# Differential heads: one split over a bank's 128 rows, with DMAs placing the quarters

## The chip, the cores and the metric

The kernel runs on one core of a Trainium2 chip. The metric is the device time of one execution in microseconds (us). Engines are named TensorE (PE in the rows; PEld is its weight load), VectorE (DVE), ScalarE (ACT), GpSimd (POOL) and SyncE (SP), which here only issues DMAs.

## The reference

One decoder layer over x of 1 x 512 x 1024 float32: RMSNorm, one input projection whose columns go to four groups of four heads (MoBA, NSA, differential, sliding window), output projection, norm, residual, then a gated feed-forward part with a short convolution. The change touches the differential heads alone:

```python
dq4 = _heads(dq, GROUP_HEADS); dk4 = _heads(dk, GROUP_HEADS)   # (b, 4, s, 64)
# q1, k1 = the first 32 of 64 columns, q2, k2 = the last 32
s1 = einsum('bhqd,bhkd->bhqk', q1, k1) * 32 ** -0.5 - slope * dist
s2 = einsum('bhqd,bhkd->bhqk', q2, k2) * 32 ** -0.5 - slope * dist
p = _masked_softmax(s1, mask) - lam * _masked_softmax(s2, mask)
o = einsum('bhqk,bhkd->bhqd', p, v)                             # then an RMSNorm per head
```

So there are eight narrow heads of 32 columns, two for each of the four heads.

## The kernel before, in words

Every float32 operand is split in two: a rounded high part and the rest. A product of two operands is three matmuls, high by high, high by low and low by high.

The attention half has two kinds of work. The heads' own steps (scores, softmax, transposes, probabilities times values) are written in an order with due times and get a high priority. The projections that later heads need are "filler": a generator, `everything`, runs `fill_moba`, `fill_nsa`, `fill_diff`, `fill_swa` and `fill_out` in this order, some pieces between any two steps of the heads. One unit of filler, `fm_unit`, takes a split weight, fills one PSUM bank with the tag "mm" (there are two such banks) by 24 matmuls of 128x512, and returns it. The bank holds 128 projected columns as rows, by 512 positions. What must be done to it on ScalarE, VectorE and by DMA goes to a queue `side`, from which steps are taken one after another as the filler goes on; `mm_bank` makes sure that the steps of the bank before last have been written down. The splits of weights (lines 152 and 157) go through the same queue. A scheduler then plans the order of instructions on each engine from priorities and from when it believes that operands and buffers are ready.

`fill_diff` makes four such banks: for p = 0 and 1, the queries of heads 2p and 2p + 1, then the keys. The 128 rows of a bank are four quarters of 32 rows, one for each narrow head. For every quarter `narrow_stack` fills a tile "dd" of 128 x 512, of which 96 rows are used: the high part twice and the low part once, in such an order that one score matmul with a depth of 96 (line 1062) adds up all three products. In the kernel before, ScalarE writes the high part of one quarter (line 828), SP issues a DMA that copies it to its second place (line 829), and VectorE writes the low part (line 833): four times for each bank. The "dd" tiles share 18 buffers with other head tiles (tag F); the "sum" tiles are two buffers that the feed-forward weights use later (line 177).

SP also issues the loads of weights (lines 91 and 104) and of the gains (line 869), in the same queue as the copies.

Of the kernel before, what the change touches and what calls it, by code (L numbers as in the profile page):

```python
# [11 lines left out]
F32 = mybir.dt.float32  # L12
BF16 = mybir.dt.bfloat16
F32R = mybir.dt.float32r
AF = mybir.ActivationFunctionType
ALU = mybir.AluOpType
AX = mybir.AxisListType

S = 512
# [10 lines left out]
def f32(ap):  # L30
    return ap.bitcast(F32)
# [199 lines left out]
def kernel(  # L231
# [6 lines left out]
    vec, act, pool, pe, sp = nc.vector, nc.scalar, nc.gpsimd, nc.tensor, nc.sync  # L238
# [4 lines left out]
    wst = ctx.enter_context(tc.tile_pool(name="wst", bufs=4))  # L243
    vpool = ctx.enter_context(tc.tile_pool(name="big", bufs=BIGS))
    first_half = ExitStack()
    tab = first_half.enter_context(tc.tile_pool(name="tab", bufs=1))
# [5 lines left out]
    def nm(s):  # L252
        cnt[0] += 1
        return f"{s}_{cnt[0]}"
# [3 lines left out]
    def bank(tag):  # L258
        if tag == "pv":
            turn[0] ^= 1  # L260
            tag = ("va", "vb")[turn[0]]
        return psum.tile([128, 512], F32, tag=tag, name=nm(tag), bufs=1 if tag[0] == "v" else 2)

    def tt(name, tag="F"):
        return acts.tile([128, S], F32R, tag=tag, name=nm(name), bufs={"F": FB, "M": MB, "H": HB}[tag])
# [17 lines left out]
    def later(*fs):  # L283
        side.extend(fs)
        asked[0] += len(fs)
# [129 lines left out]
    for n in range(2):  # L415
        ps = bank("sc")
        for _ in range(WARM[n]):
            keep(pe.transpose(ps[:, 0:128], ident, ident))
        if n == 0:
            ps = bank("tr")  # L420
# [39 lines left out]
    def mm_done():  # L460
        marks.append(asked[0])

    def fm_unit():
        w = W.take()
        ps = mm_bank()
        yield from fm_pieces(ps, w, hT, slice(0, S))
        W.free()
        return ps
# [65 lines left out]
    def qscale(m, h, dim):  # L534
        return float(-np.float64(dim) ** -0.5 / np.float64(SLOPES[4 * h + m]))
# [59 lines left out]
    ps = bank("tr")  # L595
# [24 lines left out]
    pool.memset(pair, 0.0)  # L620
    pool.memset(pair[0:64, 0:1], 1.0)
    pool.memset(pair[64:128, 1:2], 1.0)
    nsink = tab.tile([128, 4], F32, name="nsink")
    keep(vec.tensor_scalar(nsink, sink, -1.0, None, ALU.mult))
    lprod = tab.tile([128, 2, 32], F32, name="lprod")
# [14 lines left out]
    nq, nk, dq, dk, sq_, sk = [], [], [], [], [], []  # L640
    vcs, cmp_, late = {}, {}, {}

    def tm_units(v, v3, n, extra=None):
        ws = [W.take() for _ in range(4)]
        for t in range(4):
            ps = mm_bank()
            sl = slice(128 * t, 128 * t + 128)
            for k in range(8):
                wh, wl = ws[k // 2]
                mm3(ps[:, 0:n], hT[0][k][:, sl], hT[1][k][:, sl], wh[:, k % 2, :], wl[:, k % 2, :], k == 0, k == 7)  # L650
                if t == 3 and k % 2:
                    W.free()
                yield 1
            later(*v_steps(ps, v, v3, t, (lambda ps=ps, t=t: extra(ps, t)) if extra else None))
            mm_done()
# [161 lines left out]
        vec.tensor_sub(ct[1], ps, f32(ct[0]))  # L817
        cmp_["v"], cmp_["p"] = vc, ct

    def narrow_stack(ps, scales, places, twice, put):  # L820


        ts_ = []

        def hi(c):
            t = tt("dd")
            ts_.append(t)
            act.activation(t[0:32], ps[32 * c:32 * c + 32, :], AF.Copy, scale=scales[c // 2])
            sp.dma_start(f32(t[twice:twice + 32]), f32(t[0:32]))

        def lo(c):
            t = ts_[c]
            vec.scalar_tensor_tensor(t[places:places + 32], ps[32 * c:32 * c + 32, :], scales[c // 2], f32(t[0:32]),
                                     ALU.mult, ALU.subtract)
            put.append(t)
        return [lambda f=f, c=c: f(c) for f, c in ((hi, 0), (hi, 1), (lo, 0), (hi, 2), (lo, 1), (hi, 3), (lo, 2), (lo, 3))]

    def fill_diff():
        for p in range(2):
            ps = yield from fm_unit()  # L840
            later(*narrow_stack(ps, [qscale(2, 2 * p + a, 32) for a in range(2)], 32, 64, dq))
            mm_done()
            ps = yield from fm_unit()
            later(*narrow_stack(ps, [1.0, 1.0], 64, 32, dk))
            mm_done()
        vcs["d"] = vpool.tile([128, 4, 512], F32R, tag="v", name="vd")
        vs = vpool.tile([128, 4, 512], F32R, tag="v", name="vs")
        vcs["s"] = vs[:, :, 0:384].rearrange("p t (n d) -> p t n d", n=2)
        yield from tm_units(vcs["d"], vcs["s"], 384)
        yield "diff"  # L850
# [37 lines left out]
    def everything():  # L888
        yield from fill_moba()
        yield from fill_nsa()  # L890
        yield from fill_diff()
        yield from fill_swa()
        yield from fill_out()
# [585 lines left out]
```

## Time and profile before

| | |
|---|---|
| median of 3 runs | 822.89 us (821.38 to 822.95) |
| the profiled execution | 821.32 us, of it 819.5 us span |
| mean granted TensorE clock | 0.984 of full speed |
| TensorE busy | 781.0 us (95% of the span) |
| VectorE busy | 665.6 us (81%) |
| ScalarE busy | 446.9 us (55%) |
| GpSimd busy | 338.5 us (41%) |

The shares are means over stages with different limits: an engine that is busy for 55% of the span can be the limit in a short stretch. The differential banks are written between 121.6 and 160.5 us, and their scores run from 159.2 to 234.3 us. Starts of instructions are microseconds from the start of the span.

### The profile page before, as it was taken

How to read it: one execution, taken by the hardware profiler on the slowest of the kernel's cores; microseconds unless marked ns; L12 is line 12 of the kernel's file. 1: busy time of each engine (PE TensorE's matmuls, PEld its weight loads, DVE VectorE, ACT ScalarE, POOL GpSimd, SP SyncE). 2: the span in 40 equal slices, each digit the busy share in tenths (PEclk: the TensorE clock that was granted, in tenths of full speed). 3: DMA queues.
4: the chain of work that ended last, by engine and by line, in shares of the span. 5: the costliest groups of instructions: out<-in, count | busy, mean ns of one | idle time of the engine just before them, and what ended most of it. 6: DMA issues, size and time to landing. Idle time of an engine off the chain costs nothing.

```text
span 819.5 us, 13505 instructions
## 1 busy us (share of the span) xinstructions
PE 781.0 (95%) x5087; PEld 712.1 (87%) x5087; DVE 665.6 (81%) x1131; ACT 446.9 (55%) x931; POOL 338.5 (41%) x309
## 2 busy tenths in 40 slices
PE   8999998999989769999999999999999999999995
PEld 8998986997868658988998998998998998998984
DVE  5657768877586999896797797897897987989857
ACT  6657666777676545645554453454454454445532
POOL 5245333336244757343343441461561561563103
PEclk9999999999989979999999999999999999999998
DMA  7455201416211403412114305216116026033212
GB/s 213 121 149 138 64 22 46 129 52 216 80 52 52 154 7 109 145 61 94 52 50 157 103 10 197 67 38 206 43 61 206 18 86 205 1 104 104 69 60 102
DMA packets 72920, 78.76 MB, mean 96 GB/s; under 512 B 7782, under 2 KB 58136, under 8 KB 72856
## 3 DMA queue, kind: packets, MB, share of 16 engines
q1 hardware_dynamic: 71032, 73.71, 29.3%
q10 hardware_dynamic: 1824, 4.20, 1.5%
q8 instruction: 40, 0.66, 0.3%
q14 instruction: 24, 0.20, 0.1%
HBM read 73.71 MB, written 2.10 MB: 93 GB/s over the span
## 4 chain that ended last, share of the span: by engine, by line
PE 57%; DVE 33%; issue 3%; DMA 3%; ACT 2%; POOL 1%; ACTq 0%; DVEq 0%; POOLq 0%
DVE wu L194 13%; PE mm L405 5%; PE mm L406 5%; PE mm L407 4%; DVE y L1362 3%; PE mm L1312 3%; PE mm L1314 3%; PE mm L1313 3%; PE tr L406 3%; PE tr L407 2%; PE sc L1314 2%; PE sc L1313 2%; PE sc L1312 2%; PE tr L405 2%; PE tr L973 2%
## 5 line engine op out<-in xcount | busy, mean ns | idle before, releaser
L194 DVE TENSOR_TENSOR wu<-pair,wu 128x512 fp32r<-128x512 f32 x188 | 174.6, 964 | 15.8 <-ACT wu L191 15.6
L191 ACT ACTIVATE wu<-pair 128x512 fp32r<-128x512 f32 x188 | 108.6, 622 | 76.3 <-PE sc L1314 19.8
L1314 PE MATMUL mm<-fT,wu 128*128 128x256 f32 x488 | 138.3, 283 | 0.7 <-DVE wu L194 0.7
L1312 PE MATMUL mm<-fT,wu 128*128 128x256 f32 x488 | 138.2, 283 | 0.7 <-ACT mo L1343 0.7
L1313 PE MATMUL mm<-fT,wu 128*128 128x256 f32 x488 | 138.2, 283 | 0.0
L1314 PE MATMUL sc<-fT,wu 128*128 128x256 f32 x392 | 111.3, 284 | 0.0
L1313 PE MATMUL sc<-fT,wu 128*128 128x256 f32 x392 | 111.1, 284 | 0.0
L1312 PE MATMUL sc<-fT,wu 128*128 128x256 f32 x392 | 111.0, 284 | 0.0
L152 ACT ACTIVATE wu<-raw 128x512 fp32r<-128x512 f32 (+2 forms) x126 | 71.3, 609 | 67.9 <-DMA raw<-in_ffn_w_down_dram 43.8
L177 POOL TENSOR_TENSOR sum<-pair 128x512 f32<-128x512 f32 x32 | 48.7, 1526 | 141.2 <-DMA pair<-in_ffn_w_up_dram 71.4
L177 POOL TENSOR_TENSOR pair<-sum,pair 128x512 f32<-128x512 f32 x32 | 56.2, 1771 | 116.6 <-DVE wu L194 114.7
L177 POOL TENSOR_TENSOR pair<-pair 128x512 f32<-128x512 f32 x64 | 103.4, 1628 | 2.0
L157 DVE TENSOR_TENSOR wu<-raw,wu 128x512 fp32r<-128x512 f32 (+2 forms) x96 | 73.5, 783 | 35.3 <-ACT wu L152 34.8
L1312 PEld LDWEIGHTS mm<-fT,wu 128*128 128x128 f32 x488 | 93.6, 192 | 1.2 <-ACT mo L1343 0.9
L1314 PEld LDWEIGHTS mm<-fT,wu 128*128 128x128 f32 x488 | 93.6, 192 | 0.9 <-DVE wu L194 0.9
L1313 PEld LDWEIGHTS mm<-fT,wu 128*128 128x128 f32 x488 | 93.6, 192 | 0.3
L941 POOL TENSOR_SCALAR P<-P,rc 128x128 f32<-128x128 f32 (+2 forms) x80 | 42.3, 547 | 84.3 <-DVE rc L1039 39.6
L1313 PEld LDWEIGHTS sc<-fT,wu 128*128 128x128 f32 x392 | 75.2, 192 | 0.3
L1312 PEld LDWEIGHTS sc<-fT,wu 128*128 128x128 f32 x392 | 75.2, 192 | 0.3
L1314 PEld LDWEIGHTS sc<-fT,wu 128*128 128x128 f32 x392 | 75.3, 192 | 0.0
L949 ACT ACTIVATE P<-P,mn 128x128 f32<-128x128 f32 (+2 forms) x96 | 52.1, 543 | 33.2 <-DVE mn L948 32.8
L157 POOL TENSOR_TENSOR wu<-raw,wu 128x512 fp32r<-128x512 f32 (+2 forms) x30 | 40.6, 1356 | 48.4 <-ACT wu L152 44.7
(318 smaller groups left out, 1955.8 us busy)
## 6 DMA issues: line engine op xcount, KB each, us to landing
pair<-in_ffn_w_gate_dram SPq DMA_DIRECT2D x16, 1024.0 KB, 7.7
pair<-in_ffn_w_up_dram SPq DMA_DIRECT2D x16, 1024.0 KB, 5.4
raw<-in_ffn_w_down_dram SPq DMA_DIRECT2D x32, 512.0 KB, 4.1
raw<-in_w_in_dram SPq DMA_DIRECT2D x14, 512.0 KB, 3.9
raw<-in_w_out_dram SPq DMA_DIRECT2D x8, 512.0 KB, 5.4
raw<-in_w_in_dram SPq DMA_DIRECT2D x10, 256.0 KB, 3.2
x<-in_x_dram SPq DMA_DIRECT2D x4, 512.0 KB, 4.6
x<-in_x_dram ACTq DMA_DIRECT2D x4, 512.0 KB
```

The lines of the kernel that those rows point to most:

```text
L152: keep(self.nc.scalar.activation(box["h"][:, sl], box["r"][:, sl], AF.Copy))
L157: keep(eng.tensor_tensor(box["l"][:, sl], box["r"][:, sl], f32(box["h"][:, sl]), op=ALU.subtract))
L177: self.nc.gpsimd.tensor_tensor(block(g, out), block(g, a), block(g, b), op=op)
L191: self.nc.scalar.activation(box["h"][g], block(g, src), AF.Copy)
L194: self.nc.vector.tensor_sub(box["l"][g], block(g, src), f32(box["h"][g]))
L405: pe.matmul(o, lh, rh, start=first, stop=False)
L406: pe.matmul(o, lh, rl, start=False, stop=False)
L407: pe.matmul(o, ll, rh, start=False, stop=last)
L949: act.activation(pi, pi, AF.Exp, bias=mn[:, i:i + 1], scale=-1.0, accum_out=sm[:, i:i + 1])
L1312: pe.matmul(o, wh, rh, start=first, stop=False, skip_group_check=True)
L1313: pe.matmul(o, wh, rl, start=False, stop=False, skip_group_check=True)
L1314: pe.matmul(o, wl, rh, start=False, stop=last, skip_group_check=True)
```

## The change

A bank is no longer split by quarters. ScalarE writes the high part of all 128 rows into a staging tile, VectorE the low part into another, and SP's DMAs carry the quarters to their places in the four "dd" tiles: eight copies of the high part and four of the low part for each bank. The staging tiles have the tag "sum". The scale of the queries differs between the two heads of a bank, so it becomes a column with a value for each row, filled by four memsets.

```diff
+    dscale = tab.tile([128, 2], F32, name="dscale")
+    for h in range(4):
+        pool.memset(dscale[64 * (h % 2):64 * (h % 2) + 64, h // 2:h // 2 + 1], qscale(2, h, 32))
...
-    def narrow_stack(ps, scales, places, twice, put):
-        ts_ = []
-
-        def hi(c):
-            t = tt("dd")
-            ts_.append(t)
-            act.activation(t[0:32], ps[32 * c:32 * c + 32, :], AF.Copy, scale=scales[c // 2])
-            sp.dma_start(f32(t[twice:twice + 32]), f32(t[0:32]))
-
-        def lo(c):
-            t = ts_[c]
-            vec.scalar_tensor_tensor(t[places:places + 32], ps[32 * c:32 * c + 32, :], scales[c // 2], f32(t[0:32]),
-                                     ALU.mult, ALU.subtract)
-            put.append(t)
-        return [lambda f=f, c=c: f(c) for f, c in ((hi, 0), (hi, 1), (lo, 0), (hi, 2), (lo, 1), (hi, 3), (lo, 2), (lo, 3))]
+    def narrow_stack(ps, scale, places, twice, put):
+        ts_ = [tt("dd") for _ in range(4)]
+        parts = [wst.tile([128, S], F32R, tag="sum", name=nm("parts"), bufs=2) for _ in range(2)]
+
+        def place(n, c, row):
+            sp.dma_start(f32(ts_[c][row:row + 32]), f32(parts[n][32 * c:32 * c + 32]))
+
+        def hi():
+            act.activation(parts[0], ps, AF.Copy, scale=scale)
+            for c in range(4):
+                place(0, c, 0)
+                place(0, c, twice)
+
+        def lo():
+            vec.scalar_tensor_tensor(parts[1], ps, scale, f32(parts[0]), ALU.mult, ALU.subtract)
+            for c in range(4):
+                place(1, c, places)
+                put.append(ts_[c])
+        return [hi, lo]
...
-            later(*narrow_stack(ps, [qscale(2, 2 * p + a, 32) for a in range(2)], 32, 64, dq))
+            later(*narrow_stack(ps, dscale[:, p:p + 1], 32, 64, dq))
...
-            later(*narrow_stack(ps, [1.0, 1.0], 64, 32, dk))
+            later(*narrow_stack(ps, 1.0, 64, 32, dk))
```

## Rows read from the trace of the kernel before

**Rows 1.** Busy time by windows: engines' busy us (instructions), PEclk, DMA share, GB/s

```profile
126.00:128.00 2.00, 0.65 (x4) 0.22 (x2) 1.94 (x3) 1.95 (x6) 1.00 (x1) 1.00 0.12 29
128.00:130.00 2.00, 1.46 (x7) 0.91 (x7) 2.00 (x8) 1.95 (x6) 0.00 (x0) 1.00 0.63 167
130.00:132.00 2.00, 1.36 (x5) 0.99 (x5) 1.96 (x5) 1.98 (x7) 0.00 (x0) 0.68 0.45 128
132.00:134.00 2.00, 1.93 (x5) 1.49 (x5) 1.91 (x8) 1.66 (x6) 0.00 (x0) 0.50 0.00 0
136.00:200.00 64.00, 64.00 (x358) 57.30 (x356) 48.63 (x124) 44.64 (x112) 31.71 (x38) 1.00 0.38 117
200.00:210.00 10.00, 8.75 (x41) 6.79 (x41) 8.00 (x22) 6.81 (x16) 2.30 (x3) 1.00 0.43 132
230.00:300.00 70.00, 53.31 (x282) 42.97 (x281) 59.59 (x130) 43.79 (x112) 38.18 (x43) 0.88 0.23 76
```

**Rows 2.** TensorE in order of time: start, us, instruction, idle before and releaser

```profile
109.66 0.47 PE L407 MATMUL mm<-hT,wu 128*128 128x512 f32 x1
...
124.68 0.39 PE L407 MATMUL mm<-hT,wu 128*128 128x512 f32 x1
...
128.19 0.33 PE L1005 MATMUL sc<-kk,qs 128*128 128x128 f32 x1 [1.54 <-DVE mn L948]
...
130.64 0.83 PE L973 MATMUL tr<-ident,P 128*128 128x128 f32 x3 [0.68 <-DVE PT L977]
...
132.18 0.79 PE L405 MATMUL mm<-hT,wu 128*128 128x512 f32 x1
```

**Rows 3.** The chain of waits around the first differential bank

```profile
123.50 0.69 DVE dd L833
...
125.94 0.68 DVE dd L833
...
130.73 0.69 DVE dd L833
131.43 0.70 DVE dd L833
```

**Rows 4.** Groups by line and form, 120 to 162 us: busy, mean ns, idle before

```profile
L828 ACT ACTIVATE dd<-mm 32x512 fp32r<-32x512 f32 x16 | 9.4, 589 | 3.2 <-DVE dd L833 2.7
...
L816 ACT ACTIVATE cmp<-vb 128x512 fp32r<-128x512 f32 x1 | 0.6, 597 | 0.0
...
L833 DVE SCALAR_TENSOR_TENSOR dd<-mm,dd 32x512 fp32r<-32x512 f32 x16 | 11.0, 687 | 2.2 <-ACT dd L828 1.8
...
L977 DVE TENSOR_TENSOR PT<-tr,PT 128x512 fp32r<-128x512 f32 x4 | 2.7, 685 | 0.3 <-ACT PT L976 0.2
```

**Rows 5.** The tile "dd": ns min/median/max, first and last start

```profile
L1062 PE MATMUL sc<-dd,dd x32: 221/338/502, 159.2 to 234.3; 96*128 96x128 f32 x8, 96*128 96x256 f32 x8, 96*128 96x384 f32 x8, 96*128 96x512 f32 x8
...
L829 SPq DMA_DIRECT2D dd<-dd x16: 507/510/609, 122.2 to 158.4; - x16
...
DMA to landing us min/median/max: 1.9/1.9/2.5
```

**Rows 6.** ScalarE in order of time

```profile
121.61 1.19 ACT L828 ACTIVATE dd<-mm 32x512 fp32r<-32x512 f32 x2
...
127.56 1.81 ACT L828 ACTIVATE dd<-mm 32x512 fp32r<-32x512 f32 x3
```

**Rows 7.** SP's DMA issues in order of time

```profile
127.61 0.91 SPq L91 DMA_DIRECT2D raw<-in_w_in_dram  x2
...
153.16 0.57 SPq L869 DMA_DIRECT2D gains<-in_attn_post_norm_dram  x1
...
158.43 0.51 SPq L829 DMA_DIRECT2D dd<-dd  x1
```

**Rows 8.** GpSimd in order of time, at the start

```profile
3.54 0.09 POOL L621 MEMSET pair<- 64x1 f32 x1
3.69 0.09 POOL L622 MEMSET pair<- 64x1 f32 x1
```

**Rows 9.** The tile "sum": ns min/median/max, first and last start

```profile
L177 POOL TENSOR_TENSOR sum<-pair x32: 1282/1664/1761, 191.0 to 747.7; 128x512 f32<-128x512 f32 x32
```

## The prediction, made before the kernel was run

> **What bounds the kernel now.** TensorE carries most of the span, so a change on other engines can only pay where TensorE stands still or runs at a lower clock. The first view is therefore the busy time by windows around the differential banks. From 136 to 200 us TensorE is busy without a gap, so that stretch can only start earlier; the exception is 126 to 134 us. There it is busy for 0.65, 1.46, 1.36 and 1.93 us of four windows of 2 us, while VectorE is busy for 1.94, 2.00, 1.96 and 1.91 us and ScalarE for 1.95, 1.95, 1.98 and 1.66 [rows 1]. For these 8 us VectorE and ScalarE are the limit and TensorE waits for them. After it the granted clock falls: 0.68 in 130 to 132 us and 0.50 in 132 to 134, which is the lower level, 1.2 GHz, after the engine had stood still for 1.54 us and again for 0.68 us [rows 1, 2].
>
> The second view, TensorE's instructions in order of time, says what TensorE waits for. It stands at 126.7 for a running minimum that VectorE has to read out before a score bank is free, at 130.6 for a split of transposed probabilities, and the projection matmul that starts at 132.18 is late too [rows 2]. The third, the chain of waits, runs through VectorE here: it holds four differential splits (line 833) of 0.69, 0.68, 0.69 and 0.70 us, the last ending at 132.13, and 0.05 us later the matmul into the next projection bank starts [rows 3]. There are two "mm" banks, and the third differential bank reuses the one that these four splits read. Its own last matmul was issued at 109.66 [rows 2], but its first evacuation starts at 121.61 [rows 6] and its last ends at 132.13: ten microseconds for eight short instructions.
>
> **The change part by part.**
>
> *Evacuations.* ScalarE loses 16 copies of 589 ns (9.4 us) and gets 4 over 128 rows. A 128x512 copy from PSUM takes 597 ns [rows 4], so 2.4 us: 7.0 us less. VectorE loses 16 splits of 687 ns (11.0 us) and gets 4; the 128x512 subtraction from PSUM takes 685 ns [rows 4], so 2.7 us: 8.3 us less. The time of one does not grow with the rows; a per-partition scale in place of a constant has no row of its own, and I take it as free (bounds: 0 and, if it doubled them, 4 x 0.6 + 4 x 0.7 = 5.2 us on engines that have idle time outside the one stretch). The ping-pong goes too: ScalarE sat idle 2.7 us for VectorE's splits of the same bank [rows 4].
>
> *What that is worth.* TensorE's loss in 126 to 134 us is idle time of 1.35 + 0.54 + 0.64 + 0.07 = 2.6 us, and at the lower clock 1.36 x 0.32 + 1.93 x 0.50 = 1.4 us: 4.0 us [rows 1]. That is the ceiling. The floor is what leaves the chain: 2.76 us of four splits become one of 0.69, so 2.1 us [rows 3]. The bank is now free after one copy and one split. With the split at the place where the first one stands now (123.50, 0.69 us long [rows 3]) that is 124.2 instead of 132.13, so 24 matmuls of the next bank, 0.23 us apart at full clock, 5.5 us of work, can stand where TensorE is idle now. Between floor and ceiling I take the middle, 3.0 us. It keeps its worth to the end: what follows is TensorE's own work until 200 us [rows 1], and the stages behind start from it. What the two engines save besides (8.3 - 2.1 = 6.2 us on VectorE, most of ScalarE's 7.0) lies behind 134 us, beside a TensorE that is full; I cost it at nothing.
>
> *The copies.* 16 transfers become 48, twelve for each bank, all issued by SP and 64 KB each. One issue takes 0.51 us of SP (median) [rows 5], so 24.5 us instead of 8.2: 16.3 us more on SP, and 2.1 MB more to move. A copy lands 1.9 us after its issue, 2.5 at most [rows 5]. Bank 1: eight copies of the first part from 122.2 to 126.3, four of the second to 128.4, the last landing by 130.9. The first score that reads such a tile runs at 159.2 [rows 5]; bank 2's would have landed by about 138 even if its first part is written as late as 128.8 (12 x 0.51 + 2.5 behind it), so 21 us are spare, and 18 if the scores come 3 us sooner: nothing. Banks 3 and 4 serve the later half of the 32 scores, the last of them at 234.3.
>
> *What stands behind them on SP.* The weight load issued at 127.61 [rows 7] goes behind bank 1's copies and is issued some 1 to 2 us later; none of the rows shows an engine waiting for a weight load in this stretch, so it costs nothing, and at most those 1 to 2 us if one comes to wait. The last differential tile gets its buffer late: its copy is issued at 158.43, and the two loads of gains went ahead of it at 153 [rows 7]. In the new kernel it is SP, not ScalarE, that waits for this buffer. The order on SP put what was ready first, and I expect that again. If the copies stood in front, only loads with nothing due for tens of microseconds would be held for up to 5 us: nothing.
>
> *The two staging tiles.* They rotate through the two "sum" buffers, which nothing else uses until 191.0 [rows 9]. That is the one new wait: a bank's first part can't be written before the eight copies of the bank ahead have landed. I cost it at nothing in the forecast and at 3.1 us and more in the staging-tile case below.
>
> *The constants.* Four memsets on GpSimd; such a one takes 0.09 us, and GpSimd does these in the first 4 us, while the first loads are under way [rows 8]: nothing, and 0.36 us without that cover.
>
> One rule speaks against the change. Copies 0.6 us apart still landed 1.9 us after their issues here [rows 5, 6], so they overlapped. The Trainium skill (DMA: Bandwidth & Descriptors, Rules for kernel authors) says to coalesce small transfers, since under 64 KB one pays mostly overhead, and that transfers to disjoint partition halves gain nothing because they share the same engines and serialize. By that rule bank 1's first eight copies, one after another, would end at 122.2 + 8 x 1.9 = 137.4 and hold up bank 2 by 12 us, so up to 835; by the rows they take 4.1 us of SP and 1.9 of landing, and the sum stands. The trace agrees with the row's reading as far as two copies in flight; eight in flight no row shows, and the staging-tile case below is the same hold-up priced by rows.
>
> **The rivals.**
>
> *Hidden: no change that can be measured.* The engines get their order from a scheduler that plans all of this anew, and TensorE could wait in the same stretch for the next thing: the softmax rows between, which VectorE must still do. For it: of the 5.4 us between 126.7 and 132.1, only 1.4 us on VectorE are differential splits; the rest is softmax, probability splits and weight work. Against it: a free "mm" bank gives TensorE work that needs none of these. It gives 822.9, within 1.65 us.
>
> *Slower: the staging tile holds up ScalarE.* Bank 2's matmuls end at about 125.1 [rows 2]. Its copy needs the buffer of bank 1's first part: copied at 121.61 to 122.2 [rows 6], eight issues of 0.51, landing 1.9: 128.2. If that copy is queued in ScalarE ahead of softmax work from 125.1, ScalarE stands 3.1 us in the stretch where it is busy 98%; VectorE's split waits for four more issues, to 130.2, where ScalarE's copy would let it run at 128.8: 1.4 us; banks 3 and 4 add 12 x 0.51 - 5.5 = 0.6 us each. Sum 3.1 to 5.7, and the gain does not come about while the engines that feed TensorE stand: 826.0 to 828.6, from 824.6 where part of the gain stays. It decides from the point where ScalarE is held for longer than the 3.0 us gained plus 1.65. For it: SP's 0.51 us per issue, twelve in a row. Against it: now the second bank's first copy starts at about 128.2 (the second of three from 127.56 [rows 6]), just when the buffer would come free, and the planner sees that a buffer is taken.
>
> *More than forecast.* The fourth bank's "mm" bank is held by a late tile now and would be free some 9 us sooner; TensorE's 1.25 idle us in 200 to 210 could go, and part of what the clock loses in 230 to 300 (53.3 x 0.12 = 6.4 us) [rows 1] changes with the order. 4.0 + 1.25 = 5.3, up to 7.9 with two fifths of the clock's loss: 817.6 down to 815.0.
>
> **How the numbers follow.** The profiled execution took 821.32 us (span 819.5, 1.8 around it); the median of the three runs is 822.89, 1.6 above. 3.0 us off gives 818.3 on the first and 819.9 on the second, which I forecast. About 0.2% (1.65 us) is what a measurement can tell from no change. Chances: the forecast, 818.8 to 820.8, 0.44; more than that, 815.0 to 818.8, 0.12; hidden, 821.3 to 824.5, 0.23; the staging tile's wait, 824.6 to 828.6, 0.21. So faster 0.56, same 0.23, slower 0.21. The range takes in the forecast, the hidden case, most of the larger gain and the staging-tile case to its middle: 816.0 to 826.5. The likeliest one's own range is 818.8 to 820.8.
>
> **What the profile after would show.** Right: four ScalarE and four VectorE instructions on 128x512 for these banks, no longer in the chain; 48 copies on SP at about 0.5 us; TensorE without the idle time of 126 to 132 us and at full clock to 136; the first differential score some 3 us sooner. Wrong: ScalarE's or VectorE's evacuation waiting for DMAs, or SP's copies landing after far more than 2.5 us (the staging-tile case); TensorE idle for as long, on other names (hidden). Also wrong: a new order that makes or unmakes a drop of the clock between 230 and 300 us, where nothing of this change runs.

## The result and the profile after

The changed kernel takes 814.31 us (median of 4 runs, 813.53 to 815.22) where the one before takes 822.85 (821.38 to 822.95): 8.5 us less, a ratio of 0.9901 with a 95% interval of 0.9884 to 0.9918. The forecast was 819.9, and its range ended at 816.0. The two profiled executions are 814.86 us (span 813.0) and 821.32 us (span 819.5), 6.5 us apart.

The windows around the differential banks, after, with the columns of [rows 1]:

```profile
126.00:128.00 2.00, 2.00 (x13) 1.74 (x12) 1.93 (x5) 1.35 (x5) 2.00 (x5) 1.00 0.00 0
128.00:130.00 2.00, 2.00 (x11) 1.56 (x11) 2.00 (x3) 0.81 (x3) 1.06 (x1) 1.00 0.00 0
130.00:132.00 2.00, 2.00 (x12) 1.58 (x11) 1.86 (x8) 1.82 (x5) 0.00 (x0) 1.00 0.76 197
132.00:134.00 2.00, 2.00 (x13) 1.74 (x12) 2.00 (x5) 0.91 (x4) 0.00 (x0) 1.00 0.36 87
136.00:200.00 64.00, 64.00 (x357) 57.26 (x356) 45.22 (x120) 44.55 (x117) 33.66 (x40) 1.00 0.52 151
200.00:210.00 10.00, 10.00 (x50) 8.36 (x49) 7.39 (x25) 6.61 (x18) 2.83 (x5) 1.00 0.15 55
230.00:300.00 70.00, 53.13 (x306) 44.71 (x306) 61.03 (x120) 38.05 (x94) 39.09 (x42) 0.90 0.21 70
```

TensorE is now busy without a gap and at full clock from 126 to 134 us, although VectorE is as full as before (1.93, 2.00, 1.86 and 2.00 of each 2 us). So VectorE's fullness was not what stopped TensorE there. The idle time of 200 to 210 us is gone too.

The groups of the evacuations by form, 110 to 155 us, answer to [rows 4]; the tile "dd" answers to [rows 5], and SP in order of time to [rows 7]:

```profile
L839 DVE SCALAR_TENSOR_TENSOR parts<-mm,dscale,parts 128x512 fp32r<-128x512 f32 x2 | 1.5, 736 | 0.0
L839 DVE SCALAR_TENSOR_TENSOR parts<-mm,parts 128x512 fp32r<-128x512 f32 x2 | 1.4, 682 | 0.0
L833 ACT ACTIVATE parts<-mm,dscale 128x512 fp32r<-128x512 f32 x2 | 1.4, 680 | 0.0
L833 ACT ACTIVATE parts<-mm 128x512 fp32r<-128x512 f32 x2 | 1.2, 585 | 0.0
```

```profile
L830 SPq DMA_DIRECT2D dd<-parts x48: 507/585/1268, 115.8 to 158.7; - x48
...
L1069 PE MATMUL sc<-dd,dd x32: 222/338/481, 159.8 to 226.0; 96*128 96x128 f32 x8, 96*128 96x256 f32 x8, 96*128 96x384 f32 x8, 96*128 96x512 f32 x8
...
DMA to landing us min/median/max: 2.0/2.5/3.7
```

```profile
115.83 7.58 SPq L830 DMA_DIRECT2D dd<-parts  x12
129.08 0.90 SPq L91 DMA_DIRECT2D raw<-in_w_in_dram  x2
131.38 8.22 SPq L830 DMA_DIRECT2D dd<-parts  x12
...
149.08 5.59 SPq L830 DMA_DIRECT2D dd<-parts  x9
154.72 0.58 SPq L876 DMA_DIRECT2D gains<-in_attn_post_norm_dram  x1
155.34 0.46 SPq L876 DMA_DIRECT2D gains<-in_ffn_pre_norm_dram  x1
157.48 1.78 SPq L830 DMA_DIRECT2D dd<-parts  x3
```

Four copies and four splits take the place of sixteen each. The last three placing copies go behind the gains, as the one late copy did before. The first differential score runs at 159.8 us, no sooner than before (159.2), but the last at 226.0 in place of 234.3.

Copies of three of the four banks (the second's, at 130.78, is shown with the third staging tile below) and the first bank's split, from ScalarE's and VectorE's instructions in order of time:

```profile
113.28 0.69 ACT L833 ACTIVATE parts<-mm,dscale 128x512 fp32r<-128x512 f32 x1
114.68 0.74 DVE L839 SCALAR_TENSOR_TENSOR parts<-mm,dscale,parts 128x512 fp32r<-128x512 f32 x1
...
138.95 0.67 ACT L833 ACTIVATE parts<-mm,dscale 128x512 fp32r<-128x512 f32 x1
...
148.46 0.60 ACT L833 ACTIVATE parts<-mm 128x512 fp32r<-128x512 f32 x1
```

The first bank is copied at 113.28, 8.3 us sooner than the 121.61 of [rows 6], and let go at 115.42, not at 132.13.

**TensorE's loss.** From here on, a stretch's loss is TensorE's idle time plus its busy time times what is missing from the granted clock, reckoned apart on each side of every step of the clock. From 100 to 136 us it was 4.3 us before and is 0; from 200 to 260 us 9.6 before (1.25 + 4.92 idle, 3.4 by the clock) and 5.7 after (0.39 + 5.35, 0); from 260 to 320 us 15.3 and 17.2. Together that is some 6.2 us. But up to 100 us the changed kernel loses 5.1 us and the one before 3.0 (a drop of the clock, last section), and behind 320 us 13.3 and 13.6. So idle time and clock explain some 4.4 of the 6.5 us between these two executions; the other 2 lie in time in which TensorE counts as busy. A second profile of the changed kernel (below) has 0 in the first stretch again, but 7.3 in the second, so the first term is firm and the split of the rest is not.

**Counted by work.** Every trace here holds the same 5087 matmuls, so one can also ask how much sooner TensorE has begun the same number of columns (an estimate from the starts of the matmuls, good to about 0.2 us, as their order differs a little). Against the kernel before, the changed one is 1.6 us behind at 120 us (the drop of the clock), then 3.6 ahead at 150 us, 3.8 at 195, 5.8 at 211 and 6.1 at 780. Its second profile, without that drop, is level at 120 us and then 5.2, 5.5, 7.4 and 7.5 us ahead. So the stretch around 126 us is worth 5.2 us in both, more than the 4.3 of idle time and clock: the ends of matmuls are modelled, and short halts between two starts count as busy. Another 2.0 us come between 195 and 211 us in both.

### The profile page after: what moved, and what is told of

The parts are those of the page before. It is cut to its first block, busy times and chain, and to the rows that moved or that the text cites. A ratio compares the mean times of both kernels' runs of the same rounds, so it can differ in the third digit from the quotient of the medians.

```text
span 813.0 us, 13542 instructions
## 1 busy us (share of the span) xinstructions
PE 776.9 (96%) x5087; PEld 710.5 (87%) x5087; DVE 658.4 (81%) x1119; ACT 439.2 (54%) x919; POOL 339.2 (42%) x313
## 4 chain that ended last, share of the span: by engine, by line
PE 63%; DVE 28%; DMA 3%; issue 3%; ACT 2%; POOL 0%; ACTq 0%; DVEq 0%; POOLq 0%; SPq 0%
DVE wu L194 11%; PE mm L405 5%; PE mm L406 5%; PE mm L407 5%; PE tr L406 3%; PE mm L1319 3%; PE mm L1321 3%; PE mm L1320 3%; PE tr L407 3%; DVE y L1369 3%; PE tr L405 3%; PE sc L1319 3%; PE sc L1321 3%; PE sc L1320 3%; PE tr L980 2%
## 5 line engine op out<-in xcount | busy, mean ns | idle before, releaser
L157 DVE TENSOR_TENSOR wu<-raw,wu 128x512 fp32r<-128x512 f32 (+2 forms) x96 | 71.7, 764 | 33.0 <-ACT wu L152 32.3
```

The source lines that it names most:

```text
L157: keep(eng.tensor_tensor(box["l"][:, sl], box["r"][:, sl], f32(box["h"][:, sl]), op=ALU.subtract))
```

## The experiments

Four theories were put against each other. **A:** the gain is engine time, the 7 and 8 us that ScalarE and VectorE no longer spend. **B:** it is how long a bank is held, at first by the hand-offs between the two engines; later, after two runs below had spoken against that form, by a point in time: TensorE runs out of other work at about 126.6 us, and a bank let go before that keeps it busy. **C:** it is the pace of the side steps, of which a bank now has two and not eight. **D:** the evacuation could not begin, because it wrote straight into "dd" tiles that had no free buffer; the staging tiles took that wait off the bank.

Each kernel was timed in 3 rounds beside the kernel before on the same chip (the last two in 5). Times are medians, and those of different rows can come from different chips; the ratios are what compares them. "Bank 1" is the first differential bank, and the losses are those of one profiled execution each.

| | us | ratio to before, 95% | bank 1 let go at | loss 100-136 | loss 200-260 |
|---|---|---|---|---|---|
| before | 822.85 | | 132.1 | 4.3 | 9.6 |
| e1_highs_first | 820.19 | 0.9978 [0.9965, 0.9992] | 127.9 | 1.5 | 7.3 |
| e5_two_more_buffers | 823.39 | 1.0014 [0.9995, 1.0034] | 127.8 | 2.0 | 11.0 |
| e11_first_bank_held | 819.51 | 0.9966 [0.9951, 0.9980] | 138.5 | 1.7 | 8.0 |
| e4_hand_offs | 816.03 | 0.9922 [0.9907, 0.9937] | 116.0 | 0.3 | 6.4 |
| e6_staged_quarters | 815.37 | 0.9916 [0.9890, 0.9942] | 121.0 | 0.3 | 4.5 |
| e7_buffer_hold | 814.80 | 0.9922 [0.9891, 0.9952] | 124.5 | 0 | 4.4 |
| after | 814.31 | 0.9901 [0.9884, 0.9918] | 115.4 | 0 | 5.7 |
| e2_idle_steps | 813.59 | 0.9895 [0.9879, 0.9911] | 115.5 | 0 | 5.7 |
| e3_engine_time | 812.97 | 0.9886 [0.9871, 0.9900] | 113.9 | 0 | 3.7 |
| e9_one_more_buffer | 812.23 | 0.9887 [0.9865, 0.9908] | 113.8 | 0 | 5.2 |
| e10_three_staging | 811.74 | 0.9867 [0.9841, 0.9893] | 115.5 | 1.7 | 4.4 |

The 1.7 us of the last row are the clock's alone (last section).

**Order of the steps alone.** The kernel before, with all four copies of a bank written down ahead of its four splits:

```diff
-        return [lambda f=f, c=c: f(c) for f, c in ((hi, 0), (hi, 1), (lo, 0), (hi, 2), (lo, 1), (hi, 3), (lo, 2), (lo, 3))]
+        return [lambda f=f, c=c: f(c) for f, c in ((hi, 0), (hi, 1), (hi, 2), (hi, 3), (lo, 0), (lo, 1), (lo, 2), (lo, 3))]
```

> The kernel before with the eight steps of a bank reordered: four high copies, then four low splits, so ScalarE no longer waits for VectorE within a bank; the same 32 instructions, 16 copies by DMA. Theory A (time on VectorE and ScalarE is what counts): as before, 822 to 824. Theory B (how long an mm bank is held counts, and the hand-offs between the two engines make most of the hold): part of the gain, 816 to 820, with the third bank's first matmul some 3 us or more before 132.18. Theory C (the steps' pace in the queue, or a chance order of the plan): any value, with no earlier release.

About 2 us faster (2.3 at the medians of the two beside each other, 1.8 by the ratio). Bank 1 is let go at 127.9, and TensorE's wait in the stretch ends with it, from TensorE's instructions in order of time:

```profile
127.99 0.50 PE L405 MATMUL mm<-hT,wu 128*128 128x512 f32 x1 [1.46 <-DVE dd L833]
```

So without any change of the work or of the transfers, the loss of this stretch goes from 4.3 to 1.5 us. But 1.7 us of idle time appear between 136 and 200 us, where there was none.

**Six empty steps behind the two.** The changed kernel:

```diff
-        return [hi, lo]
+        return [hi, lo] + [lambda: None] * 6
```

> The changed kernel with six empty steps behind the two of each bank, so that a bank takes eight places of the side queue as before. Theories A and B: 813 to 816, as the changed kernel. Theory C: 3 us or more of the 8.5 us gained are lost, 817 to 823.

Nothing is lost; C falls.

**The engines' time given back.** The changed kernel, with three copies on ScalarE and three subtractions on VectorE for each bank, on 32 rows of the staging tiles, their results unused:

```diff
+        def spend():
+            t = ta("spend", 1)
+            act.activation(t[0:32], f32(parts[0][0:32]), AF.Copy)
+            vec.tensor_sub(t[32:64], f32(parts[1][32:64]), f32(parts[0][32:64]))
+        return [hi, lo, spend, spend, spend]
```

> The changed kernel, and for each bank three more 32x512 copies on ScalarE and three more 32x512 subtractions on VectorE, from the staging tiles into a tile that nothing reads: the engines' time of before (12 x 0.59 and 12 x 0.69 us), with the mm bank released as in the changed kernel. Theory A: the gain is lost, 820 to 823. Theory B: 814 to 816.5. Theory C: no statement.

By form, 110 to 160 us:

```profile
L847 DVE TENSOR_TENSOR spend<-parts,parts 32x512 f32<-32x512 f32 x12 | 9.3, 774 | 0.4
L846 ACT ACTIVATE spend<-parts 32x512 f32<-32x512 f32 x12 | 7.4, 620 | 4.1 <-DVE spend L847 4.1
```

Both engines do what the change had saved them, and the kernel is no slower (812.97). A falls as a matter of the sum over the four banks. Little of the added work lies in 126 to 134 us itself: the first bank's runs at 113 to 118 us, and one copy and one subtraction start in that stretch. That its load did not decide there either is shown by VectorE, full after the change beside a full TensorE, and by the staged quarters below, which have all 32 instructions back.

**The hand-offs given back.** The changed kernel, with six tiny reads of the bank (32x8, `a` on ScalarE, `d` on VectorE) in the old order, results unused:

```diff
-        return [hi, lo]
+        return [hi, a, lo, a, d, a, d, d]
```

> The changed kernel, and for each bank three reads of 32x8 by ScalarE and three by VectorE from the mm bank, in the order of the steps of before (high, high, low, high, low, high, low, low), into tiles that nothing reads: hardly any engine time (12 x 0.2 and 12 x 0.15 us), but the bank is held until the last of them, through the same hand-offs. Theory B: most of the gain is lost, 818 to 823, TensorE idle again near 130 us. Theory A: 814 to 816. Theory C: no statement.

1.7 us slower than the changed kernel by the ratios, with intervals that overlap, and not the loss that B expected of the hand-offs. The tiny reads hold bank 1 for only some 2 us beyond its split, to 116.0, so this tests a short hold.

**Two buffers more for the first quarters.** The kernel before, with the first two of its sixteen "dd" tiles in the two "sum" buffers:

```diff
+            if put is dq and not dq and c < 2:
+                t = wst.tile([128, S], F32R, tag="sum", name=nm("dd"), bufs=2)
+            else:
+                t = tt("dd")
```

> The kernel before, with the first two differential tiles in the two buffers of the tag sum instead of two of the 18 of tag F; everything else as before, quarters and hand-offs included. Theory D (a bank's evacuation could not begin because the tiles that it wrote had no free buffer, and the staging tile took that wait off the bank): the first bank's first copies some 8 us sooner, the fourth bank let go sooner, and a part of the gain, 816 to 821. Theory B (hand-offs): 821 to 823.

ScalarE and VectorE on the first bank, in order of time:

```profile
111.80 1.20 ACT L831 ACTIVATE dd<-mm 32x512 fp32r<-32x512 f32 x2
...
122.08 0.59 ACT L831 ACTIVATE dd<-mm 32x512 fp32r<-32x512 f32 x1
...
126.40 1.39 DVE L836 SCALAR_TENSOR_TENSOR dd<-mm,dd 32x512 fp32r<-32x512 f32 x2
```

Two buffers move two copies to 111.80, ten microseconds forward, and the third, which has none, to 122.08 only. So D names rightly what made the evacuation begin late. But it buys nothing by itself: the bank is let go at 127.8, TensorE stands 1.09 us for it and 1.11 us for the next bank at 136.18, and the time is that of before. Counted by work, this kernel is 2.7 us ahead of the one before at 150 us, much as with the order alone (3.1), and 2.6 behind at 225: a gain in this stretch need not keep to the end.

**Staged, but in quarters.** The changed kernel's staging tiles and 48 copies, with the sixteen copies, the sixteen splits and the hand-off order of before (`rows(a, c)` is the quarter c of a):

```diff
+        def hi(c):
+            act.activation(rows(parts[0], c), rows(ps, c), AF.Copy, scale=of(c))
+            place(0, c, 0)
+            place(0, c, twice)
...
+        return [lambda f=f, c=c: f(c) for f, c in ((hi, 0), (hi, 1), (lo, 0), (hi, 2), (lo, 1), (hi, 3), (lo, 2), (lo, 3))]
```

> The changed kernel with its staging tiles and 48 copies by DMA, but split by quarters in the order of before: 16 copies of 32x512 on ScalarE, 16 splits on VectorE, with the hand-offs between them. Theory D: nearly all of the gain stays, 813 to 817. Theory B: most of it is lost, 818 to 823. Theory A is refuted already where engine time alone was added; by it 820 to 823.

Nearly the whole gain is there with all 32 instructions and their ping-pong, against what B expected of the hand-offs: what counts is that the bank, begun at 113.37, is let go by 121.0, not how many instructions that takes.

**The buffers' wait put back.** The changed kernel, with a tiny write from the bank (32x8) into an unused corner of each "dd" tile ahead of the bank's copy, so that ScalarE waits for the "dd" buffers again while the bank is held:

```diff
+            for c in range(4):
+                act.activation(ts_[c][96:128, 0:8], ps[96:128, 0:8], AF.Copy)
```

> The changed kernel; ahead of a bank's high copy, ScalarE writes 32x8 values from the bank into an unused corner of each of its four differential tiles, so that the bank is held until all four have a free buffer, as before; hardly any engine time (16 x 0.15 us), one hand-off per bank. Theory D: most of the gain is lost, 818 to 824. Theory B: 813 to 816.

ScalarE and VectorE:

```profile
122.63 0.36 ACT L834 ACTIVATE dd<-mm 32x8 fp32r<-32x8 f32 x4
123.01 0.69 ACT L835 ACTIVATE parts<-mm,dscale 128x512 fp32r<-128x512 f32 x1
...
123.73 0.75 DVE L841 SCALAR_TENSOR_TENSOR parts<-mm,dscale,parts 128x512 fp32r<-128x512 f32 x1 [0.22 <-ACT parts L835]
...
158.48 0.69 DVE L841 SCALAR_TENSOR_TENSOR parts<-mm,parts 128x512 fp32r<-128x512 f32 x1
```

TensorE's window, with the columns of [rows 1]:

```profile
100.00:136.00 36.00, 36.00 (x219) 31.43 (x219) 28.25 (x96) 24.99 (x78) 12.40 (x19) 1.00 0.24 61
```

The evacuation begins as late as before the change (122.6), but now takes 1.5 us, and the bank is free at 124.5: no loss from 100 to 136 us, and the gain stays (814.80, with a wide spread of 812.78 to 817.75). It also holds the fourth bank to 159.2, nearly as late as before (160.5), without harm that shows. So the early start (D) is one way to let the bank go before 126.6, and the short evacuation is another; either is enough.

**The first bank held, all else as changed.** A tiny read of bank 1 waits for its last placed quarter, and two small round trips by DMA follow before the last read:

```diff
+        def hold():
...
+            vec.tensor_add(t[32:64], ps[32:64, 0:8], f32(ts_[3][32:64, 0:8]))
+            for _ in range(2):
...
+                sp.dma_start(u[32:64], t[32:64])
...
+                vec.tensor_add(t[32:64], ps[32:64, 0:8], u[32:64])
+        return [hi, lo, hold] if first else [hi, lo]
```

> The changed kernel, with only its first differential bank held longer: a tiny read of the bank waits for the last placed quarter to land, and two small round trips over a DMA and VectorE follow before a last tiny read. It should let the bank go at about 129 to 132 us, in place of 115.4, and costs VectorE less than 0.5 us. Theory B (TensorE stands whenever the first bank is released after about 126.6 us): 3 to 4.5 us of TensorE's loss come back between 126 and 134 us. If the rest of the gain (behind 200 us) follows from that first stall, the time is 819.5 to 822; if it comes from the later banks by itself, 816.5 to 819. If the release of this bank does not decide, 813 to 815.5, with no loss in 100 to 136 us.

Windows of 2 us, TensorE's waits in order of time, and the differential scores (the lines of this kernel are shifted by 11):

```profile
128.00:130.00 2.00, 1.44 (x10) 1.13 (x10) 2.00 (x8) 2.00 (x7) 1.98 (x3) 1.00 0.00 0
130.00:132.00 2.00, 1.56 (x9) 0.88 (x8) 2.00 (x10) 2.00 (x7) 0.00 (x0) 1.00 0.43 94
132.00:134.00 2.00, 1.42 (x7) 0.93 (x8) 1.94 (x8) 2.00 (x7) 0.00 (x0) 1.00 0.58 169
```

```profile
128.39 0.33 PE L991 MATMUL tr<-ident,P 128*128 128x128 f32 x1 [0.49 <-POOL P L959]
...
133.57 0.50 PE L405 MATMUL mm<-hT,wu 128*128 128x512 f32 x1 [0.41 <-DVE parts L839]
```

```profile
L1080 PE MATMUL sc<-dd,dd x32: 221/338/475, 163.1 to 235.1; 96*128 96x128 f32 x8, 96*128 96x256 f32 x8, 96*128 96x384 f32 x8, 96*128 96x512 f32 x8
```

The picture of before comes back: VectorE and ScalarE full, TensorE at 1.4 to 1.6 of 2 us, waiting for softmax rows and transposes, until a projection bank is free at 133.5 (the second bank's; the first is held to 138.5, longer than meant). The last differential score is at 235.1, as before the change. 5.2 of the 8.5 us are lost (819.51), just inside the "rest of the gain follows" outcome, although the stretch itself shows a loss of only 1.7 us where 3 to 4.5 were expected. Counted by work, with the same clock in both up to 240 us, this kernel is level with the changed one at 120 us and 3.3 us behind it at 150: 1.7 of idle time, and the rest in halts too short to show as idle. It is 5.7 us behind at 211 us. So B holds, in the form of the point in time. The second and the third bank were not held by themselves.

**One buffer more for the tag of the "dd" tiles**, in the changed kernel (`FB = 19` for 18):

> The changed kernel with 19 buffers in place of 18 for the tag that the dd tiles use. If what holds the staging tiles is the copies that wait for a dd buffer, one more lets the second bank's copy start some 3 us sooner, as three staging tiles did, and the time is 811 to 813. If it is SP's pace of 0.6 us an issue, the second bank's copy stays at about 130 us and the time is 813.5 to 815.5.

812.23, inside the first range, but not by its mechanism: the second bank's copy starts at 129.10, not 130.78, and the third's at 137.28, not 138.95. But its first bank starts sooner by the same 1.7 us (111.62), and the second profile of the unaltered changed kernel (the next experiment) has 111.73, 129.21 and 137.40. So the buffer moves nothing; the profile shown above started its banks late, after a drop of the clock at 85 to 95 us (last section).

**A third staging tile.** The changed kernel with three "sum" buffers:

```diff
-            ... tag="sum", name=nm("parts"), bufs=2) for _ in range(2)]
+            ... tag="sum", name=nm("parts"), bufs=3) for _ in range(2)]
```

> The changed kernel with three buffers of tag sum instead of two, so that a bank's high copy need not wait for the copies out of the one ahead (in the changed kernel the second bank is copied at 130.8 us). If the staging tile holds a bank up: 1 to 3 us faster than the changed kernel, 811 to 813.5. If not: 813.5 to 815.5.

ScalarE's four copies:

```profile
113.40 0.69 ACT L833 ACTIVATE parts<-mm,dscale 128x512 fp32r<-128x512 f32 x1
127.61 0.58 ACT L833 ACTIVATE parts<-mm 128x512 fp32r<-128x512 f32 x1
135.61 0.67 ACT L833 ACTIVATE parts<-mm,dscale 128x512 fp32r<-128x512 f32 x1
143.08 0.58 ACT L833 ACTIVATE parts<-mm 128x512 fp32r<-128x512 f32 x1
```

With the first bank at the same place, the second is copied 3.2 us sooner, the third 3.3 and the fourth 5.4. The staging tiles did hold these copies up, though no copy of the changed kernel stands in the trace as waiting for a DMA: the second bank's copy comes four activations further back in ScalarE's order, most likely because the plan counts the tile as taken, and ScalarE was idle for 1.19 us ahead of it on other business:

```profile
127.98 0.47 ACT L983 ACTIVATE PT<-tr 128x384 fp32r<-128x384 f32 x1
129.64 0.63 ACT L800 ACTIVATE cp<-cp 128x512 f32<-128x512 f32 x1 [1.19 <-DVE cp L799]
130.18 0.60 ACT L956 ACTIVATE P<-P,mn 128x384 f32<-128x384 f32 x1
...
130.78 0.57 ACT L833 ACTIVATE parts<-mm 128x512 fp32r<-128x512 f32 x1
```

The two kernels were run once more side by side:

> The changed kernel as it is, beside the one with three staging tiles on the same chip. 0.988 to 0.992 of the kernel before.

> The changed kernel with three staging tiles in place of two, beside the unaltered one on the same chip. If the wait of ScalarE's copies for a staging tile costs time, 1.5 to 3 us less than the changed kernel, with intervals that do not overlap; if the first comparison was chance, within 1 us of it.

The changed kernel: 813.16 (812.77 to 814.71), 0.9887 [0.9868, 0.9906]. With three staging tiles: 811.42 (810.80 to 812.08), 0.9860 [0.9840, 0.9880]. 1.7 us; no run of the one reaches into those of the other, here or in the first pair (which did not stand side by side), but the intervals of the ratios overlap, and the kernel with one more "dd" buffer, whose copies move nowhere, came to 812.23. By its median it is the fastest version found, 11 us below the kernel before. How the earlier copies save the time is not shown: counted by work, neither pair of profiles has the kernel with three tiles ahead before 211 us.

## Why the prediction was wrong

**What bounds the kernel: right in place, half right in cause.** TensorE's loss of 126 to 134 us is where the largest firm part of the gain came from, and the held "mm" bank was the reason. The windows read as "VectorE and ScalarE are the limit" were not: with 9.3 and 7.4 us of work given back to them nothing is lost, and after the change VectorE is as full as before while TensorE is full too. VectorE was late only with the instructions that TensorE needed because it had no projection to do.

**The step that failed: "between floor and ceiling I take the middle, 3.0 us".** The mechanism was right, the term was mis-sized. The floor counted the splits that leave VectorE's chain; but engine time has no price here, so that floor was the wrong measure. What decides is a point in time: the bank let go at 124.2 by the prediction's own working, before TensorE runs dry at 126.7. The kernel with the buffers' wait put back does just that (124.5), and the whole loss of the stretch goes: where 3.0 us were forecast, 4.3 us of idle time and clock are measured against a ceiling of 4.0, and 5.2 counted by work. A release on the right side of such a point earns all of the stretch; those at 127.8 and 127.9 leave 2.0 and 1.5 us.

**The second part of it: "it keeps its worth to the end", and nothing more behind 134 us.** It kept it and grew: 8.5 us at the medians. That more could come was the "more than forecast" case, at a chance of 0.12 with 815.0 to 818.8; the result lies 0.7 us beyond its end. Its mechanism, the fourth bank freed sooner, is not what did it: with that bank held to 159.2 us the gain stays. The first bank did: holding it alone takes 5.2 us away, and puts the last differential score back from 226.0 to 235.1. It is worth more than the 1.7 us that TensorE then idles beside it for two reasons. The first is short halts in time that counts as busy (3.3 us by work). The matmuls themselves last longer, too: the 42 score matmuls of one line between 100 and 265 us last 369 ns before and 343 after, groups by line,

```profile
L1005 PE MATMUL sc<-kk,qs 128*128 128x256 f32 (+3 forms) x42 | 15.4, 369 | 3.1 <-DVE mn L948 3.0
```

```profile
L1012 PE MATMUL sc<-kk,qs 128*128 128x256 f32 (+3 forms) x42 | 14.3, 343 | 2.7 <-DVE mn L955 2.6
```

and 356 with the first bank held (the lower clock, for 10 us in the one and 3.4 us in the other, can have a part in both). The second is a stall behind 200 us, which the sum left out (its 1.25 us stand in the rival alone); TensorE in order of time before, and with the first bank held:

```profile
204.38 0.44 PE L973 MATMUL tr<-ident,P 128*128 128x128 f32 x2 [0.22 <-DVE P L1082]
205.79 0.47 PE L405 MATMUL mm<-wu,mixh 128*128 128x512 f32 x1 [0.98 <-DVE kl L504]
```

```profile
205.27 0.44 PE L991 MATMUL tr<-ident,P 128*128 128x128 f32 x2 [1.23 <-DVE P L1100]
```

Both stand for the probabilities of a differential head (lines 1082 and 1100), or for a later "mm" bank that VectorE (line 504) splits just behind them. In both profiles of the changed kernel TensorE has no idle time from 200 to 210 us. That is where the 2 us between 195 and 211 us come from. What is left, about 1 us between 211 and 260 us, is not settled: the clock stood at its lower level from 239.9 to 246.8 us before (3.4 us lost), never there in one profile of the changed kernel, and for 3.4 us in the other (1.7 lost), and no run separates that from the rest.

**A cause not foreseen: the late start.** The prediction put the first copy where it stood, at 121.6, and asked only how long the evacuation takes. The copy stood there because a "dd" buffer was missing; a staging tile needs none, and it moved to 113.28. That was not needed for the gain, but it gives the release 11 us of room.

**The copies.** The count and the order on SP were right, the durations low: twelve in a row took 7.58 us, 0.63 each, in place of 0.51, and landed 2.5 us after issue (3.7 at most), in place of 1.9 (2.5). (The trace gives the landing of only a dozen of the 48.) To the scores it cost nothing, as argued: the first comes at least 16 us after the second bank's copies have landed. The rule that speaks against the change (the Trainium skill, DMA: Bandwidth & Descriptors, Rules for kernel authors: transfers to disjoint partition halves share the same engines and serialize) would have put the landing of eight copies 15.2 us behind the first issue (8 x 1.9, an estimate); the trace agrees only so far as issue and landing grew by a quarter and a third, and with the longest landing seen the eighth copy is down some 8 us behind the first issue.

**The staging tile's wait.** The tiles do hold up the second bank's copy, but as a later place in ScalarE's order and not as an engine that stands. That the size agrees (3.1 us predicted, 3.2 measured with the third tile) is luck: all twelve copies out of the first bank's tiles were issued by 123.4 us and, by the longest landing seen, down by 127.1, over 3 us before the second bank's copy ran at 130.78. And it did not decide. The rival had it end in a stretch where the engines feed a TensorE that has nothing else; with the first bank free TensorE had its projections, and the later copies cost at most about 1.7 us of a larger gain.

**The constants** were costed at nothing, and are nearly that: a per-row scale lengthens ScalarE's copy from 585 to 680 ns and VectorE's split from 682 to 736, 0.3 us in all. The first differential score "some 3 us sooner" did not come about (159.8, and 158.3 in the second profile, against 159.2); the gain shows at the last score (226.0 and 224.4, against 234.3). That the heads' order sets the first one's place is likely, but no run shows it.

## What to carry to other kernels

Where TensorE stands beside full engines, ask first which buffer it would need to have work of its own, when that buffer is let go, and when TensorE runs dry. A release before that point cost next to nothing here, however close (124.5: 0), and one behind it cost more the later it came (127.9: 1.5, 132.1: 4.3 us); engine time had no price. An evacuation that writes into a scarce destination holds its source bank for as long as the destination is missing; a staging tile moves that wait to a DMA queue that has time. Then count the staging tiles against their copies' landing: here a third one may be worth up to 1.7 us, where the saved instructions were worth nothing that could be measured.

## What was not expected of the hardware

The granted clock can fall while TensorE has no gap at all. The kernel with three staging tiles, in windows of 4 us:

```profile
100.00:104.00 4.00, 4.00 (x21) 3.51 (x21) 3.43 (x12) 3.23 (x9) 1.28 (x1) 0.64 0.38 100
104.00:108.00 4.00, 4.00 (x18) 3.27 (x18) 2.23 (x13) 1.18 (x5) 1.86 (x4) 0.93 0.00 0
108.00:112.00 4.00, 4.00 (x26) 3.40 (x24) 1.29 (x5) 1.94 (x8) 0.20 (x1) 1.00 0.00 0
```

TensorE is busy for 4.00 of 4 us and gets 0.64 of full speed, a mean over its two levels. Its last idle time before that, as far as the modelled ends show, was 0.86 us at 47 us; short halts would not show. The drop costs 1.7 us, in the fastest kernel of all; the profile of the changed kernel has the like, 0.83 in two windows of 5 us from 85 to 95 us, and its second profile has not (1.00 from 60 to 100 us).
